# Diagonal softmax on one core: the first load split by partitions, an early normalization, one store fewer

## Chip, core and metric

The kernel runs on one core of a Trainium2 chip. The metric is the device time of one execution in microseconds (us). Lower is better.

## The reference

`x` and `y` are float32 tensors of shape 8 x 4096 x 512. For each of the 8 batches the reference takes the diagonal of `x @ y.T`, that is 4096 dot products of 512 elements, and a softmax over those 4096 numbers.

```python
gram = np.matmul(x, y.transpose(0, 2, 1))
diag = np.diagonal(gram, axis1=1, axis2=2)
diag = diag - diag.max(axis=-1, keepdims=True)
exp = np.exp(diag)
return (exp / exp.sum(axis=-1, keepdims=True)).astype(np.float32)
```

Only the diagonal is needed, so the kernel forms 32,768 dot products and no matrix product. Its inputs are 2 x 67.1 MB, its output is 0.13 MB.

## The kernel before

**Tiling.** Four batches make a "set"; there are two sets. Within a set each batch takes 32 partitions, so partition `p` holds 128 consecutive rows of one batch, as `C = 128` columns of a set. A step takes `R = 32` of these columns: one tile of 128 partitions x 32 rows x 512 elements of `x`, and the same of `y`. A partition's part of such a tile is 64 KB that lie next to each other in memory; the tile is 8.39 MB. Steps 0 to 3 cover the first set and steps 4 to 7 the second.

**Buffers.** There are two tiles for `x` (`xs[0]` and `xs[1]`, used in turn), one for `y` (`ys`), and a small one, `side`, to which ScalarE (ACT) copies the last `K = 6` rows of `ys`.

**A step of the main loop** (`t` = 0 to 5). The SP queue issues the loads of `x` (line 63) and of `y` (line 66). Line 123 has ACT copy the last six rows of `y` to `side`. VectorE (DVE) multiplies the first 26 rows in place (line 70, `products`), then the six rows from `side` (line 70 again), and sums 30 of the 32 rows (line 73). ACT sums the other two (line 78). `ys` is free for the next `y` as soon as the first product and ACT's copy are done; an `xs` tile is free when the sums are done.

**The softmax of a set.** `exps` takes each partition's largest dot product (line 97), the largest over the batch's 32 partitions (line 91), and the exponentials with their sums on ACT (line 104). `normalize` adds up those sums over the batch (line 91), takes the reciprocal (line 110) and scales `res` (line 111). The exponentials of the first set come at the end of step 3. Its `normalize` stands in step 4, between the first and the second product.

**The end.** Step 6 loads `y` in two halves; step 7 loads `x` and `y` in pieces of 16, 8, 4, 2 and then 1 rows and forms its dot products row by row on DVE (line 83). Line 156 then stores the first set from the SP queue in five pieces, of 32, 32, 32, 16 and 16 partitions. ACT's queue stores the second set with line 158, which is the last thing that the kernel does.

**Order.** The schedule is written out by hand: each engine's instructions run in the order of the program. SP issues 31 transfers and ACT one. Each transfer takes the next of eight completion semaphores in turn, so a transfer is also held until the one eight places ahead of it has landed.

Of the kernel before, what the change touches and what calls it, by code (L numbers as in the profile page):

```python
# [1 line left out]

# [5 lines left out]


@with_exitstack
def kernel(
    ctx: ExitStack,
    tc: tile.TileContext,
    x: bass.AP,
    y: bass.AP,
    out: bass.AP,
):
    nc = tc.nc
    ctx.enter_context(tc.manual_schedule())  # L20
    f32 = mybir.dt.float32
    Alu = mybir.AluOpType
    Act = mybir.ActivationFunctionType
    X = mybir.AxisListType.X
    B, N, D = x.shape
    P = nc.NUM_PARTITIONS
    G = 32
    Q = P // G
    C = N // G
    R = 32  # L30
    H = R // 2
    K = 6
    W = 2
    S = B // Q * (C // R)


    xv = x.rearrange("(s b) (j c) d -> s (b j) c d", b=Q, j=G)
    yv = y.rearrange("(s b) (j c) d -> s (b j) c d", b=Q, j=G)
    ov = out.rearrange("(s b) (j c) -> s (b j) c", b=Q, j=G)

    big = ctx.enter_context(tc.tile_pool(name="big", bufs=1))
    small = ctx.enter_context(tc.tile_pool(name="small", bufs=1))


    xs = [big.tile([P, R, D], f32, name=f"xs{i}") for i in range(2)]
    ys = big.tile([P, R, D], f32, name="ys")
    side = big.tile([P, K, D], f32, name="side")

    diag = [small.tile([P, C + i], f32, name=f"diag{i}") for i in range(B // Q)]
    res = [small.tile([P, C], f32, name=f"res{i}") for i in range(B // Q)]  # L50

    def columns(t, r0, n):
        c0 = t % (C // R) * R + r0
        return slice(c0, c0 + n)

    def rows(t, r0, n):
        return xs[t % 2][:, r0 : r0 + n, :]

    def dots_of(t, r0, n):
        return diag[t * R // C][:, columns(t, r0, n)]  # L60

    def load_x(t, r0, n):
        nc.sync.dma_start(out=rows(t, r0, n), in_=xv[t * R // C, :, columns(t, r0, n), :])  # L63

    def load_y(t, r0, n):
        nc.sync.dma_start(out=ys[:, r0 : r0 + n, :], in_=yv[t * R // C, :, columns(t, r0, n), :])  # L66

    def products(t, r0, n, yt):
        xt = rows(t, r0, n)
        nc.vector.tensor_tensor(out=xt, in0=xt, in1=yt, op=Alu.mult)  # L70

    def sums(t, r0, n):
        nc.vector.tensor_reduce(out=dots_of(t, r0, n), in_=rows(t, r0, n), axis=X, op=Alu.add)  # L73

    def sums_act(t, r0, n):
        for r in range(r0, r0 + n):
            row = xs[t % 2][:, r, :]
            nc.scalar.activation(out=row, in_=row, func=Act.Copy, accum_out=dots_of(t, r, 1))  # L78

    def dots(t, r0, n):  # L80
        for r in range(r0, r0 + n):
            xt = xs[t % 2][:, r, :]
            nc.vector.scalar_tensor_tensor(  # L83
                out=xt, in0=xt, scalar=1.0, in1=ys[:, r, :], op0=Alu.mult, op1=Alu.mult,
                accum_out=dots_of(t, r, 1),
            )

    def over_quadrant(name, column, op, negate=False):

        got = small.tile([P, 1], f32, name=name)  # L90
        nc.vector.tensor_reduce(  # L91
            out=got, in_=column.to_broadcast([P, G]), axis=X, op=op, negate=negate, apply_transpose=True
        )
        return got

    def largest(out, d):
        nc.vector.tensor_reduce(out=out, in_=d, axis=X, op=Alu.max)  # L97

    def exps(i, d):
        mxp = small.tile([P, 1], f32, name=f"mxp{i}")  # L100
        largest(mxp, d)
        nmx = over_quadrant(f"nmx{i}", mxp, Alu.max, negate=True)
        sump = small.tile([P, 1], f32, name=f"sump{i}")
        nc.scalar.activation(out=res[i], in_=diag[i][:, :C], func=Act.Exp, bias=nmx, scale=1.0, accum_out=sump)  # L104
        return sump

    def normalize(i, sump):
        total = over_quadrant(f"sum{i}", sump, Alu.add)
        rc = small.tile([P, 1], f32, name=f"rc{i}")
        nc.vector.reciprocal(out=rc, in_=total)  # L110
        nc.vector.tensor_single_scalar(out=res[i], in_=res[i], scalar=rc, op=Alu.mult)  # L111

    nc.vector.addr_align(128, offset=0, max_nops=0)
    nc.scalar.addr_align(128, offset=0, max_nops=0)
    nc.sync.drain()  # L117
    nc.sync.drain()  # L118

    for t in range(S - 2):  # L120
        load_x(t, 0, R)
        load_y(t, 0, R)
        nc.scalar.activation(out=side, in_=ys[:, R - K :, :], func=Act.Copy)  # L123
        products(t, 0, R - K, ys[:, : R - K, :])
        if t == C // R:
            normalize(0, sump)
        products(t, R - K, K, side)
        sums(t, 0, R - W)
        sums_act(t, R - W, W)
        if t == C // R - 1:  # L130
            sump = exps(0, diag[0])

    t = S - 2
    load_x(t, 0, R)
    for r0 in (0, H):
        load_y(t, r0, H)
        products(t, r0, H, ys[:, r0 : r0 + H, :])
    sums(t, R - H // 2, H // 2)
    sums_act(t, 0, R - H // 2)

    t += 1
    r0 = 0
    for n in (16, 8, 4, 2, 1, 1):
        if r0 < R - 1:
            load_x(t, r0, max(n, 2))
        load_y(t, r0, n)
        if r0 == R - 2:
            largest(diag[1][:, C:], diag[1][:, : C - 2])
        dots(t, r0, n)
        r0 += n  # L150

    met = small.tile([P, C - R], f32, name="met")
    nc.scalar.activation(out=met, in_=diag[1][:, : C - R], func=Act.Copy)  # L153

    for p, n in ((0, G), (G, G), (2 * G, G), (3 * G, G // 2), (3 * G + G // 2, G // 2)):
        nc.sync.dma_start(out=ov[0, p : p + n, :], in_=res[0][p : p + n, :])
    normalize(1, exps(1, diag[1][:, C - 2 :]))
    nc.scalar.dma_start(out=ov[1], in_=res[1])


# [1 line left out]
_INS = ['x', 'y']  # L162
_OUTS = [((8, 4096), 'float32')]


# [23 lines left out]
```

## Time and profile before

| What | Value |
|---|---|
| Median of 3 runs | 320.84 us (320.61 to 320.96) |
| The profiled execution's own time | 320.94 us |
| Its span in the profile | 319.2 us |
| VectorE busy | 244.7 us (77%) |
| ScalarE busy | 42.0 us (13%) |
| SP's transfer queue (q1), share of 16 DMA engines' span | 97.7% |
| Read from HBM | 134.22 MB, 421 GB/s over the span |
| Instructions | 305 |

The span runs from the first recorded event of the program to the last, and 1.74 us of the execution's time lie outside it. "Busy" is the time in which an engine had an instruction running. A DMA queue's share is the time that its packets took on the 16 DMA engines, over 16 spans. Times inside the span are counted from its start.

### The profile page before, as it was taken

Reading aid. Unit: us, or ns where it says so; the run is one execution under the profiler, and the core shown is the slowest. Engines: PE = TensorE matmul, PEld = TensorE weight load, DVE = VectorE, ACT = ScalarE, POOL = GpSimd, SP = SyncE. Lnnn points to the kernel's source line nnn. Section 1 sums busy time; section 2 is a strip of 40 time slices with the busy share of each in tenths; the row PEclk is TensorE's granted clock in tenths of the full one; section 3 lists DMA queues with packets and bytes.
Section 4 is the critical chain, followed back from the end, with each engine's and each line's share of the span. In section 5 each row is a group of like instructions: output and inputs, shape, how many; then the busy total and the mean of one; then the engine's idle time right before and its main releaser. Section 6 shows DMA issues by size and latency. Waiting matters only on the chain.

```text
span 319.2 us, 305 instructions
## 1 busy us (share of the span) xinstructions
DVE 244.7 (77%) x96; ACT 42.0 (13%) x84; POOL 0.2 (0%) x4
## 2 busy tenths in 40 slices
DVE  0000069995799949999399994999949999996995
ACT  1000030100301003010020103001030100197000
POOL 0000000000000000000000000000000000000000
DMA  9999999999999999999999999999999899999993
GB/s 372 419 394 476 444 394 460 452 402 394 501 419 394 476 444 394 427 485 402 394 501 419 394 476 444 394 452 460 402 394 485 382 435 435 427 435 413 421 413 113
DMA packets 4098, 134.37 MB, mean 421 GB/s; under 512 B 512, under 2 KB 768, under 8 KB 1408
## 3 DMA queue, kind: packets, MB, share of 16 engines
q1 hardware_dynamic: 3952, 134.29, 97.7%
q10 hardware_dynamic: 144, 0.07, 0.1%
q14 instruction: 2, 0.02, 0.0%
HBM read 134.22 MB, written 0.13 MB: 421 GB/s over the span
## 4 chain that ended last, share of the span: by engine, by line
DMA 62%; DVE 35%; issue 2%; SPq 0%; ACT 0%; DVEq 0%
DMA ys<-in_y_dram 62%; DVE xs L70 30%; DVE diag L73 4%; DVE xs L83 0%; SPq L63 0%; DVE res L111 0%; DVE sum L91 0%; DVE nmx L91 0%; ACT res L104 0%; DVE rc L110 0%; DVE mxp L97 0%; DVEq L70 0%; SPq L66 0%; SPq L118 0%; SPq L117 0%
## 5 line engine op out<-in xcount | busy, mean ns | idle before, releaser
L70 DVE TENSOR_TENSOR xs<-xs,ys 128x13312 f32<-128x13312 f32 (+1 forms) x8 | 101.4, 12689 | 67.6 <-DMA ys<-in_y_dram 67.6
L73 DVE TENSOR_REDUCE diag<-xs 128x30 f32<-128x15360 f32 (+1 forms) x7 | 101.3, 14477 | 0.2
L78 ACT ACTIVATE xs<-xs 128x512 f32<-128x512 f32 x36 | 22.2, 616 | 111.7 <-DVE xs L70 111.7
L123 ACT ACTIVATE side<-ys 128x3072 f32<-128x3072 f32 x6 | 16.6, 2763 | 123.6 <-DMA ys<-in_y_dram 123.6
L83 DVE SCALAR_TENSOR_TENSOR xs<-xs,ys 128x512 f32<-128x512 f32 x32 | 20.0, 686 | 3.2 <-DMA ys<-in_y_dram 3.2
L70 DVE TENSOR_TENSOR xs<-xs,side 128x3072 f32<-128x3072 f32 x6 | 20.1, 3352 | 0.0
L78 ACT ACTIVATION_READ_ACCUMULATOR xs<-xs 128x1 f32 x36 | 6.7, 186 | 0.0
L104 ACT ACTIVATE res<-diag,nmx 128x128 f32<-128x128 f32 x2 | 0.8, 402 | 37.5 <-DVE nmx L91 37.5
L83 DVE DVE_READ_ACCUMULATOR xs<-xs,ys 128x1 f32 x32 | 2.6, 81 | 0.0
L123 ACT ACT_TABLE_LOAD x1 | 1.3, 1283 | 1.2 <-PEq L173 1.2
L91 DVE TRANSPOSE_TENSOR_REDUCE sum<-sump 128x1 f32<-128x32 f32 x2 | 0.4, 208 | 0.6 <-ACT res L104 0.6
L111 DVE TENSOR_SCALAR res<-res,rc 128x128 f32<-128x128 f32 x2 | 0.6, 288 | 0.1
L97 DVE TENSOR_REDUCE mxp<-diag 128x1 f32<-128x128 f32 (+1 forms) x2 | 0.4, 221 | 0.1
L91 DVE TRANSPOSE_TENSOR_REDUCE nmx<-mxp 128x1 f32<-128x32 f32 x2 | 0.4, 211 | 0.1
L110 DVE RECIPROCAL rc<-sum 128x1 f32<-128x1 f32 x2 | 0.3, 164 | 0.1
L104 ACT ACTIVATION_READ_ACCUMULATOR res<-diag,nmx 128x1 f32 x2 | 0.4, 187 | 0.0
L97 DVE TENSOR_REDUCE diag<-diag 128x1 f32<-128x126 f32 x1 | 0.3, 284 | 0.1
L153 ACT ACTIVATE met<-diag 128x96 f32<-128x96 f32 x1 | 0.3, 283 | 0.0
L173 POOL MEMSET const-bfloat16-1.0<- 128x1 bf16 x1 | 0.1, 103 | 0.0
L173 POOL MEMSET const-uint8-127<- 128x1 uint8 x1 | 0.1, 102 | 0.0
L173 POOL MEMSET const-float32-0.0<- 128x1 f32 x1 | 0.1, 100 | 0.2 <-issue 0.2
L173 POOL MEMSET const-float32-1.0<- 128x1 f32 x1 | 0.1, 99 | 0.0
## 6 DMA issues: line engine op xcount, KB each, us to landing
ys<-in_y_dram SPq DMA_DIRECT2D x3, 4096.0 KB, 16.0
xs<-in_x_dram SPq DMA_DIRECT2D x1, 4096.0 KB, 14.9
xs<-in_x_dram SPq DMA_DIRECT2D x1, 2048.0 KB, 20.5
ys<-in_y_dram SPq DMA_DIRECT2D x1, 2048.0 KB, 17.2
xs<-in_x_dram SPq DMA_DIRECT2D x1, 1024.0 KB, 19.3
ys<-in_y_dram SPq DMA_DIRECT2D x1, 1024.0 KB, 21.3
xs<-in_x_dram SPq DMA_DIRECT2D x2, 512.0 KB, 22.9
ys<-in_y_dram SPq DMA_DIRECT2D x1, 512.0 KB, 22.9
```

Source lines behind the costliest of these rows:

```text
L70: nc.vector.tensor_tensor(out=xt, in0=xt, in1=yt, op=Alu.mult)
L73: nc.vector.tensor_reduce(out=dots_of(t, r0, n), in_=rows(t, r0, n), axis=X, op=Alu.add)
L78: nc.scalar.activation(out=row, in_=row, func=Act.Copy, accum_out=dots_of(t, r, 1))
L83: nc.vector.scalar_tensor_tensor(out=xt, in0=xt, scalar=1.0, in1=ys[:, r, :], op0=Alu.mult, op1=Alu.mult, accum_out=dots_of(t, r, 1),)
L91: nc.vector.tensor_reduce(out=got, in_=column.to_broadcast([P, G]), axis=X, op=op, negate=negate, apply_transpose=True)
L97: nc.vector.tensor_reduce(out=out, in_=d, axis=X, op=Alu.max)
L104: nc.scalar.activation(out=res[i], in_=diag[i][:, :C], func=Act.Exp, bias=nmx, scale=1.0, accum_out=sump)
L110: nc.vector.reciprocal(out=rc, in_=total)
L111: nc.vector.tensor_single_scalar(out=res[i], in_=res[i], scalar=rc, op=Alu.mult)
L123: nc.scalar.activation(out=side, in_=ys[:, R - K :, :], func=Act.Copy)
L153: nc.scalar.activation(out=met, in_=diag[1][:, : C - R], func=Act.Copy)
L173: nc = _bacc.Bacc("TRN2", target_bir_lowering=False, num_devices=1)
```

## The change

The load of `x` for step 0 becomes two transfers from SP: 16 partitions (0 to 15), then the other 112. The first set's `normalize` moves ahead of step 4's first product. The first set is stored in four pieces of 32 partitions, where it was three of 32 and two of 16. The number of transfers stays 32.

```diff
     for t in range(S - 2):
-        load_x(t, 0, R)
+        if t:
+            load_x(t, 0, R)
+        else:
+
+            for p, n in ((0, 16), (16, P - 16)):
+                nc.sync.dma_start(out=xs[0][p : p + n], in_=xv[0, p : p + n, :R, :])
         load_y(t, 0, R)
         nc.scalar.activation(out=side, in_=ys[:, R - K :, :], func=Act.Copy)
-        products(t, 0, R - K, ys[:, : R - K, :])
         if t == C // R:
             normalize(0, sump)
+        products(t, 0, R - K, ys[:, : R - K, :])
         products(t, R - K, K, side)
...
-    for p, n in ((0, G), (G, G), (2 * G, G), (3 * G, G // 2), (3 * G + G // 2, G // 2)):
+    for p, n in ((0, G), (G, G), (2 * G, G), (3 * G, G)):
         nc.sync.dma_start(out=ov[0, p : p + n, :], in_=res[0][p : p + n, :])
```

In the changed file lines 123, 156 and 158 become 128, 161 and 163, and the two transfers of step 0's `x` are line 126.

## The prediction

> **What bounds the kernel now.** I read the DMA part of the page first, because the kernel reads 134 MB and does little with each byte.
>
> ```profile
> DMA  9999999999999999999999999999999899999993
> q1 hardware_dynamic: 3952, 134.29, 97.7%
> HBM read 134.22 MB, written 0.13 MB: 421 GB/s over the span
> ```
>
> Every slice but the last has the 16 DMA engines busy. Next comes the chain that ended last, in order of time (start, length, what):
>
> ```profile
> 1.28 41.38 DMA ys<-in_y_dram
> 42.77 14.04 DVE xs L70
> 56.88 24.49 DMA ys<-in_y_dram
> ...
> 294.40 19.24 DMA ys<-in_y_dram
> 313.66 1.36 DVE xs L83 x4
> ```
>
> The chain names DVE for 35%, but no transfer waits for it. The timeline of SP's queue shows why:
>
> ```profile
> 0.83 0.39 SPq L63 DMA_DIRECT2D xs<-in_x_dram  x1
> 1.28 0.42 SPq L66 DMA_DIRECT2D ys<-in_y_dram  x1
> 1.75 0.43 SPq L63 DMA_DIRECT2D xs<-in_x_dram  x1
> 56.88 0.33 SPq L66 DMA_DIRECT2D ys<-in_y_dram  x1
> 76.32 0.33 SPq L63 DMA_DIRECT2D xs<-in_x_dram  x1
> ...
> 304.19 7.86 SPq L156 DMA_DIRECT2D out_dram<-res  x5
> ```
>
> Step 1's x, issued at 1.75, takes 60.3 to land (the longest x in the view of that tensor), so until 62.05. Step 1's y was issued at 56.88, 5.2 ahead of that, and lands at 81.37; step 2's x was issued at 76.32, 5.05 ahead. The engines always hold the next work. One tile lasts 81.37 - 62.05 = 19.3, or 8.39 MB / 19.3 = 434 GB/s. So a microsecond that the slowest DMA engine loses anywhere is a microsecond at the end, and time that DVE gains is not.
>
> The trace's single DMA packets tell more. A partition's row of a tile is one packet of 65,536 bytes, and in the steady part it takes 2.42, which is 27.1 GB/s for one engine and 433 for 16. The engines start one after another: the first packets begin between 1.87 and 3.13 and take 2.66 to 3.31, so they end between 4.85 and 5.94. From there each engine's packets follow with no gap. By the last 64 KB packets the order of the engines is another: single slow packets, of up to 2.96 near 235, have moved some of the early ones back.
>
> [...] 496 packets of 4 bytes, 31 transfers by 16, and at the end the last engine has 2, 2, 2, 1 and 1 packets of 512 bytes for the five stores. So 16 partitions put one row on each of 16 engines, and 112 put seven. [...] Nothing in this trace shows a large load to so few partitions[...].
>
> **The change, part by part.**
>
> *Normalization moved.* It is three DVE instructions, 0.21 + 0.16 + 0.29 = 0.66:
>
> ```profile
> 193.07 0.40 ACT L104 ACTIVATE res<-diag,nmx 128x128 f32<-128x128 f32 x1 [15.55 <-DVE nmx L91]
> 193.38 0.19 ACT L104 ACTIVATION_READ_ACCUMULATOR res<-diag,nmx 128x1 f32 x1
> 197.57 14.03 DVE L70 TENSOR_TENSOR xs<-xs,ys 128x13312 f32<-128x13312 f32 x1 [4.59 <-DMA ys<-in_y_dram]
> 211.51 0.21 DVE L91 TRANSPOSE_TENSOR_REDUCE sum<-sump 128x1 f32<-128x32 f32 x1
> ```
>
> It now runs from about 193.6, when ACT's sums are there, to 194.3, in the 4.59 in which DVE waits for step 4's y. Behind it in DVE's order stands only that product, which y holds anyway. It leaves the stretch from 211.51 to 212.15, so the release of step 6's x, issued at 231.76, comes 0.64 earlier, but y is in flight until 236.2: nothing gained. Cost 0; without the idle stretch it would be at most 0.66 of DVE time inside the 5 us lead, still 0.
>
> *Stores.* One issue of 0.31 on SP goes. SP's stores wait for loads eight places back and stand behind the last loads in the engines' order; the end is set by the second set's store (ACT, issued 316.77, landing after 1.6). Per engine one semaphore packet of 0.009 goes. The bounds are -0.1 and +0.1; I take 0. The semaphores shift by one for all later loads, with the extra one in front, so no load waits for another one than before. The first product waits for a third semaphore, at most 0.05 within the 5 us lead.
>
> *The split.* SP issues one transfer more, about 0.45 from start to start, ahead of step 0's y and step 1's x. Both then queue behind 19 us of x, so 0. What counts is the engines:
>
> - Gain: with one row per engine, later engines need not wait while eight rows are set up for earlier ones, if that is what staggers them. It is at most 5.94 - 4.85 = 1.09, at least 0.
> - Loss in the first transfer: [...] A packet then takes 4 x 2.42 = 9.68 in place of 2.42, +7.3 for every engine[...] since DMA is the limit to the end, this is never made up.
> - Loss in the second: seven rows per engine. If they are consecutive (partitions 16 + 7e to 22 + 7e for engine e)[...]. The trace shows no 112-partition load: bounds 0 and 9.7, and I take 4.8.
>
> [...] 7.3 + 4.8 - 1.0 (the stagger vanishes in packets of 9.7) = +11.1. The profiled execution took 320.94 (span 319.2 and 1.74 around it), so 332.0, and 0.1 less against the median of the runs: 331.9. This case's own range is 326.5 to 338: 7.3 - 1.1 at the low end[...].
>
> **Rivals.**
>
> - *The engines bind[...]: not slower.* Place: the first transfer. If 16 packets to partitions 0 to 15 take about 3 as before, only the gain is left. Of the 1.09, late packets in mid-run hide part: I take 0.4, so 320.4, range 319.8 to 321.2. For it: 27.1 GB/s is as well an engine's rate, and the stores from 32 partitions run at the same 27 ns a packet as the last store from 128. Against: those are 512 bytes each[...]. It decides from a first packet under about 3.5 us.
> [...]
> - *Rows dealt in turn.* If the 112 rows go to engines one at a time, [...] x takes 77 in place of 19: about 378. A 128-partition load dealt so would run at a quarter of what the trace shows, so this is unlikely.
> - *The split does not act*: if DMA had slack, any of this would be hidden. The SP timeline excludes it.
>
> **Chances.** [...] rows in turn 0.03, engine-bound 0.36. About 0.2% (0.64 us) is what a measurement of this kernel tells from no change. Engine-bound splits into 0.12 faster, 0.21 within, 0.03 slower[...]. In all: faster 0.12, same 0.21, slower 0.67. The range must reach down to the engine-bound case[...]: 319.9 to 338.0, leaving out about 0.1.
>
> **What would show it.** Right: the chain's first piece, step 0's y, ends near 53 in place of 42.67, all later pieces are shifted by the same amount, first packets take near 9.7, and the first slices of the GB/s row fall far below 372. Then DVE busy stays at 244.7 and its idle time before line 70 grows by some 11. The normalization shows at some 194 plus the shift. Wrong: first packets of about 3 and step 0's y landing near 42[...].

## The result and the profile after

The changed kernel takes 341.92 us (median of 6 runs, 341.5 to 342.2); beside it the kernel before took 320.73 us (6 runs, 320.46 to 320.96). The ratio is 1.066, with a 95% interval of 1.0646 to 1.0673: 21.2 us slower. The sign was forecast, the size was not: 331.9 was said, with 338.0 as the upper end.

The DMA part of the page of the changed kernel:

```profile
DMA  9989989898999999999999999999999999999992
GB/s 125 246 239 246 239 377 485 377 485 377 485 385 470 400 462 400 462 400 454 416 447 416 454 431 439 408 454 408 454 424 447 416 408 435 431 431 412 426 411 102
q1 hardware_dynamic: 3952, 134.29, 97.7%
HBM read 134.22 MB, written 0.13 MB: 395 GB/s over the span
```

The bytes and packets are the ones of before, and the engines are as "busy" as before: 97.7%, now of a longer span. What tells is the GB/s row: its first five slices are 125 to 246, where they were 372 to 476 in the kernel before:

```profile
GB/s 372 419 394 476 444 394 460 452 402 394 501 419 394 476 444 394 427 485 402 394 501 419 394 476 444 394 452 460 402 394 485 382 435 435 427 435 413 421 413 113
```

A DMA engine counts as busy while its packet is slow: in experiment 3 the DMA share is 0.94 at 111 GB/s, where the kernel before has 1.00 at 434.

The windows view shows the same in rates (the last column; the one ahead of it is the DMA share). It counts a packet in the window in which it starts, so that a short window has some error. First the kernel before, then the changed one:

```profile
2.00:10.00 8.00, 0.00 (x0) 0.44 (x1) 0.00 (x0) 1.00 1.06 435
11.00:40.00 29.00, 0.00 (x0) 0.00 (x0) 0.00 (x0) 1.00 1.00 434
60.00:300.00 240.00, 211.72 (x44) 37.41 (x80) 0.00 (x0) 1.00 1.00 432
```

```profile
2.00:10.00 8.00, 0.00 (x0) 0.44 (x1) 0.00 (x0) 1.00 0.90 115
11.00:40.00 29.00, 0.00 (x0) 0.00 (x0) 0.00 (x0) 1.00 0.92 224
60.00:300.00 240.00, 210.82 (x25) 25.43 (x33) 0.00 (x0) 1.00 1.00 431
```

So there is a stretch at about a quarter of the rate (the 16 partitions), a longer one at about half (the 112), and from 60 us on nothing has changed. The chain that ended last, of the changed kernel:

```profile
0.80 63.10 another core or an unknown queue
...
64.03 14.04 DVE xs L70
78.07 0.02 SPq L66
...
78.14 24.46 DMA ys<-in_y_dram
...
315.66 19.20 DMA ys<-in_y_dram
...
334.96 1.32 DVE xs L83 x4
```

The first piece carries the name of no transfer; the waits view names the one that came last (waits in total, their number, the longest). First the kernel before, then the changed one:

```profile
DVE xs L70 <- DMA ys<-in_y_dram: 67.6, 6, 42.8
```

```profile
DVE xs L70 <- DMA ys<-in_y_dram: 88.1, 6, 64.0
```

The longest of these waits was 42.8 and is 64.0. The first product starts at 64.03 where it started at 42.77, the last dots at 334.96 where they started at 313.66: 21.26 and 21.30. The whole loss is there before the first product.

The timeline of the changed kernel around step 4 shows the moved normalization:

```profile
214.58 0.19 ACT L104 ACTIVATION_READ_ACCUMULATOR res<-diag,nmx 128x1 f32 x1
214.80 0.21 DVE L91 TRANSPOSE_TENSOR_REDUCE sum<-sump 128x1 f32<-128x32 f32 x1 [0.62 <-ACT res L104]
215.04 0.16 DVE L110 RECIPROCAL rc<-sum 128x1 f32<-128x1 f32 x1
215.24 0.28 DVE L111 TENSOR_SCALAR res<-res,rc 128x128 f32<-128x128 f32 x1
218.83 14.03 DVE L70 TENSOR_TENSOR xs<-xs,ys 128x13312 f32<-128x13312 f32 x1 [3.31 <-DMA ys<-in_y_dram]
```

It lies in DVE's idle time, which ends with step 4's y as before.

The trace names no engine for a packet, but a packet starts where the one ahead of it on its engine ends, so the packets can be put in 16 rows. The single 64 KB packets, averaged over the 16 engines by their place in the order (us):

| Packet of an engine | before | after |
|---|---|---|
| 1st (in the split: the transfer of 16) | 2.96 | 8.40 |
| 2nd to 8th, added up (the transfer of 112) | 16.94 | 30.95 |
| these seven one by one, after the change | | 5.24, 4.78, 3.27, 3.80, 4.50, 4.75, 4.60 |
| 9th (the first of step 0's y) | 2.42 | 3.16 |
| 10th to 16th, each | 2.42 | 2.42 |

That is +5.4, +14.0 and +0.7, together 20.2 (before rounding) in the mean of the engines. The slowest engine ends y at 63.35 where it ended at 42.22, +21.1; the engines have also come further apart.

### The profile page after: what moved, and what is told of

It is laid out like the page before. It is cut to its first block, busy times and chain, and to the rows that moved or that the text cites. A ratio compares the mean times of both kernels' runs of the same rounds, so it can differ in the third digit from the quotient of the medians.

```text
span 340.4 us, 306 instructions
## 1 busy us (share of the span) xinstructions
DVE 244.7 (72%) x96; ACT 42.0 (12%) x84; POOL 0.2 (0%) x4
## 3 DMA queue, kind: packets, MB, share of 16 engines
q1 hardware_dynamic: 3952, 134.29, 97.7%
## 4 chain that ended last, share of the span: by engine, by line
DMA 46%; DVE 32%; another core or an unknown queue 19%; issue 2%; ACT 0%; DVEq 0%; SPq 0%
DMA ys<-in_y_dram 46%; DVE xs L70 28%; DVE diag L73 3%; DVE xs L83 0%; DVE res L111 0%; DVE nmx L91 0%; DVE sum L91 0%; ACT res L104 0%; DVE rc L110 0%; DVE mxp L97 0%; DVEq L70 0%; SPq L66 0%; DVEq L115 0%; DVEq L83 0%
```

## The experiments

The kernels change the part that loads step 0's x; all else is as in the changed kernel unless it is said. The times of the kernel before beside them were 320.55 to 320.76. Experiments 1 and 2 rest on 4 to 12 runs each, those from 3 on on one run each, and these are read by their packets as well as by their times. In the expectations theory P says that the partitions which a transfer writes set its pace, theory H that the rows which it reads do.

**1. Which of the three edits it is.** The split taken back, the other two edits kept:

```diff
-        if t:
-            load_x(t, 0, R)
-        else:
-
-            for p, n in ((0, 16), (16, P - 16)):
-                nc.sync.dma_start(out=xs[0][p : p + n], in_=xv[0, p : p + n, :R, :])
+        load_x(t, 0, R)
```

> The changed kernel with step 0's x in one transfer again; the moved normalization and the four stores stay. Theory 'the split is the whole loss': within 0.5 us of the kernel before (320.7). Rival 'the moved normalization or the stores have a share': above 321.5.

Measured: 320.59 us against 320.55, ratio 0.9998 (0.9989 to 1.0007). The moved normalization and the four stores together change nothing that can be measured.

And the split alone, put into the kernel before (the same `if`, with the normalization and the five stores of before):

> The kernel before with the split of step 0's x alone: the normalization stays between the two products and the stores stay five. If the split is the whole loss: 341.9, as the changed kernel. If the other two edits hide or add anything beside it: off by more than 0.5 us.

Measured: 341.74 us, ratio 1.0655 (1.0638 to 1.0673). The split is the whole loss.

**2. A second transfer by itself.** The same number of transfers, but cut along the rows of the tile, so that both reach all 128 partitions:

```diff
-            for p, n in ((0, 16), (16, P - 16)):
-                nc.sync.dma_start(out=xs[0][p : p + n], in_=xv[0, p : p + n, :R, :])
+            for r, n in ((0, 4), (4, R - 4)):
+                load_x(t, r, n)
```

> Step 0's x in two transfers again, but cut along the rows of the tile: 4 of the 32 rows for all 128 partitions, then the other 28. Theory P: [...] within 0.6 us of the kernel before (320.6). Rival 'a second transfer in front costs by itself': above 322.

Measured: 320.72 us against 320.66, ratio 1.0003 (0.9995 to 1.0012). One more transfer in front costs nothing; it is the cut by partitions that does.

**3. Destination or source.** Step 0's x in eight transfers of 16 consecutive partitions (from here on the diffs show only the added lines; they stand in place of the two lines of the split):

```diff
+            for p in range(0, P, 16):
+                nc.sync.dma_start(out=xs[0][p : p + 16], in_=xv[0, p : p + 16, :R, :])
```

> Step 0's x in eight transfers of 16 consecutive partitions. Theory P[...]: every packet takes about 8.3 us as the first 16 did in the changed kernel, 66 us for this x in place of 19.4, so about 321 + 47 = 368. Theory H (source rows at a pitch of 256 KB collide in memory): the same here. Rival 'only the first transfer of a program is slow': about 327 or less.

The same with partitions eight apart, at both ends:

```diff
+            for p in range(8):
+                nc.sync.dma_start(out=xs[0][p::8], in_=xv[0, p::8, :R, :])
```

> Step 0's x in eight transfers of 16 partitions that stand eight apart (0, 8, 16, ... then 1, 9, ...); the source rows are then 2 MB apart. Theory P: [...] packets of about 4.3 us, 34 us for this x, total about 336. Theory H: no relief by the destination; with the source further apart at a power of two, packets of 8 us or more, total 365 or more, or, if the wider pitch happens to be good, 2.4 us and 321.

And the source rows of the second with the destinations of the first:

```diff
+            for p in range(8):
+                nc.sync.dma_start(out=xs[0][16 * p : 16 * p + 16], in_=xv[0, p::8, :R, :])
```

> Eight transfers to 16 consecutive partitions, but from source rows 2 MB apart, so that rows of x land in other partitions than those of y and the output is another one. Theory P: like eight consecutive transfers, packets of about 8.3 us, total about 368. Theory H: like the spread transfers, whatever these take.

Measured: 374.73, 342.19 and 375.83 us. The windows view of the three, in this order, over most of the stretch in which x is loaded:

```profile
11.00:75.00 64.00, 0.00 (x0) 0.00 (x0) 0.00 (x0) 1.00 0.94 111
```

```profile
8.00:42.00 34.00, 0.00 (x0) 0.00 (x0) 0.00 (x0) 1.00 0.92 191
```

```profile
11.00:75.00 64.00, 0.00 (x0) 0.00 (x0) 0.00 (x0) 1.00 0.96 110
```

With other source rows and the same destinations the rate is the same, 111 and 110; with the same source rows and other destinations it is 191. So the partitions written decide. After the first, packets take 9.20 us with 16 consecutive partitions (9.29 with the other source rows) and 4.9 to 5.1 with the spread ones. All three totals come out 6 to 8 us above the expectations; the 8.3 us in two of them had been taken from the first packets of a program, which are shorter (8.40 in the mean, in the changed kernel). 16 packets in 9.20 us are 114 GB/s, about a quarter of the 433 of packets of 2.42.

**4. Halves.** Two transfers of 64 partitions:

```diff
+            for p in range(0, P, 64):
+                nc.sync.dma_start(out=xs[0][p : p + 64], in_=xv[0, p : p + 64, :R, :])
```

> Step 0's x in two transfers of 64 partitions. Theory P: [...] packets of 4.8 to 5.1 us, 39 to 41 us for this x in place of 19.4, total 340 to 342. Rival 'only transfers of 16 or of an odd 112 are slow': 321 to 323.

Measured: 341.85 us, most packets 5.12. The windows view of this run:

```profile
8.00:42.00 34.00, 0.00 (x0) 0.00 (x0) 0.00 (x0) 1.00 0.90 185
```

The view has 185 in a window of few packets; 16 packets in 5.12 us are 205, about half of 433. Two transfers of disjoint halves cost 21 us for one tile here.

**5. Which rows of the 112 go to which engine.** Call the packets that have the same place in the order on all 16 engines a round. If engine e has the seven consecutive partitions from 16 + 7e, its first rows are partitions 16, 23, ..., 121, its second ones 17, 24, ..., and so on. These sets, each named by its first partition, can be loaded one by one:

```diff
+            nc.sync.dma_start(out=xs[0][0:16], in_=xv[0, 0:16, :R, :])
+            for p in range(16, 23):
+                nc.sync.dma_start(out=xs[0][p::7], in_=xv[0, p::7, :R, :])
```

> Partitions 0 to 15 as in the changed kernel, then the other 112 in seven transfers of 16, of every seventh partition (16, 23, ..., 121, then 17, 24, ... and so on). Theory C (in the 112-partition load engine e has the seven consecutive rows from 16 + 7e, so these seven transfers are its seven rounds): the same packet times round by round, about 5.3, 4.7, 3.0, 3.7, 4.4, 4.7, 4.5[...]; total about 342. Rival 'the rows are dealt in another order': a different pattern, and a total that differs by several us.

Measured: 341.93 us, against 341.92 for the changed kernel. The mean packets of the seven rounds are 5.27, 4.67, 3.33, 3.73, 4.61, 4.65 and 4.46, the pattern of the changed kernel. This fits rows dealt in runs of seven that follow each other. The two short rounds are sets 18 and 19, and in the changed kernel two engines stand out in each: in the third round of the 112 they take 4.79 and 4.81 beside 2.68 to 3.31 of the other fourteen, in the fourth two others take 4.41 and 4.42 beside 3.59 to 3.73. Call such two engines a slow pair. A load of all 128 partitions can't be dealt in such runs: with eight consecutive partitions for each engine its rounds would be the sets of partitions eight apart of experiment 3, which took 4.9 to 5.1, and its packets take 2.42.

The same destinations with other source rows (`in_=xv[0, 16 + 16 * p : 32 + 16 * p, :R, :]` for the set that begins at 16 + p):

> The same destinations as in the run with seven transfers of every seventh partition, but the source rows of each of the seven are 16 that follow each other (so x stands in other partitions than y and the output is another one). Theory 'the destinations decide': the same packet times round by round, total about 342. Rival 'in these rounds memory decides': another pattern, total off by several us.

Measured: 342.66 us, with the same pattern (mean packets of 5.35, 4.69, 3.28, 3.86, 4.67, 4.73 and 4.59). Here too the destinations decide.

**6. Who pays beside the slow pair.** Transfers of 96 and 32 partitions (`((0, 96), (96, 32))` in place of `((0, 16), (16, P - 16))`):

> Step 0's x in transfers of 96 and 32 partitions. Theory C with slowed bystanders[...]: six rounds[...], about 4.5 us each, then two rounds[...], 4.8 to 5.1: 37 us for this x, total about 338. Rival [...] the colliding engines alone take 4.84 in a round, the others 2.42, and most engines get through the first six rounds in under 20 us.

Measured: 340.82 us. From the second round on every engine's packets take 4.8 to 5.1, where about 4.5 was expected up to the sixth; no engine keeps 2.42.

Is that so with one slow pair as well? In the step-7 runs the rounds of sets 18 and 19 had followed two in which all engines are slow (means of 5.27 and 4.67). So three tiles (step 0's x and y, step 1's x) were loaded set by set, each set three times in a row, sets 18 and 19 first. Of the edit, the loads that take the place of these three tiles' own:

```diff
+            for p in (18, 19, 16, 17, 20, 21, 22):
+                nc.sync.dma_start(out=xs[0][p::7], in_=xv[0, p::7, :R, :])
+                nc.sync.dma_start(out=ys[p::7], in_=yv[0, p::7, :R, :])
+                nc.sync.dma_start(out=xs[1][p::7], in_=xv[0, p::7, R : 2 * R, :])
+            nc.sync.dma_start(out=xs[0][0:16], in_=xv[0, 0:16, :R, :])
+            nc.sync.dma_start(out=ys[0:16], in_=yv[0, 0:16, :R, :])
+            nc.sync.dma_start(out=xs[1][0:16], in_=xv[0, 0:16, R : 2 * R, :])
```

> The tiles of step 0's x and y and step 1's x each in seven transfers of every seventh partition and one of 16 consecutive, ordered so that the same set of 16 partitions is loaded three times in a row: first the two sets[...] (18 and 19)[...], then partitions 0 to 15. Theory 'bystanders are slowed': also in a second and third round of one set, [...] total about 320.6 + 3 x 21.2 = 384. Rival '[...] the long packets of the others were carried over from the round before': the others fall to 2.42 in second and third rounds, and one pair alone is left at 4.8.

Measured: 402.08 us. The total is 18 above 384 because step 1's x now lands before the first product starts, at 125.5: nothing is left in the queue until the next y is issued at 139.6, and the page's GB/s row falls to 13 and 0 in two slices. The packets answer the question against the first theory, as far as one slow pair goes. In the second and third round of set 18, fourteen engines take 2.42 us and only one pair 4.88 and 4.95. But then the fourteen go on to set 19, while that pair is still on set 18: now two pairs are slow at once, and the twelve others take 4.1 a packet, until the first pair is through at 16.8; the next packet takes 2.47, and only set 19's own pair still needs 4.9.

The same with set 16 in front, `(16, 18, 19, 17, 20, 21, 22)`:

> As the run that loads each set of 16 partitions three times in a row, but the first set is 16, 23, ..., 121, [...] nothing is carried over from an earlier set. Theory 'two pairs at once slow every engine': the twelve engines [...] take about 4.1 to 4.9 us in the second and third round too. Rival 'it was the mixture of two sets that slowed them': they take 2.42 in the second and third round[...]. Total about 400 either way.

Measured: 402.23 us. In the second and third round of set 16 all sixteen engines take 5.01; when they come to set 18, fourteen of them fall to 2.43. The windows view shows it: first the run that begins with set 18 (5 to 9.5 us), then the one that begins with set 16 (6 to 15 us).

```profile
5.00:9.50 4.50, 0.00 (x0) 0.00 (x0) 0.00 (x0) 1.00 1.08 437
```

```profile
6.00:15.00 9.00, 0.00 (x0) 0.00 (x0) 0.00 (x0) 1.00 1.12 233
```

The second window is short; 16 packets in 5.01 us are 209 GB/s. Set 18 alone costs its own pair (the others 2.42), set 19 alone does too (the others 2.47), and both at once bring the twelve others to 4.1: here it is the number of slow pairs that counts, not which one. Whether set 16 holds two such pairs is not shown: at 5.01 for all sixteen none stands out. Why the others are held up is open: no trace here shows the path between an engine and the partitions it writes.

## Why the prediction was right and wrong

- *DMA sets the end, and lost time is not made up*: right. 21.26 us late at the first product, 21.30 at the last dots, and 431 GB/s in between. "No transfer waits for it" is put too short, though: in the kernel before, SP's line 66 waits 160.1 us for DVE before it issues the loads of y. What holds is that they are issued some 5 us (5.2 for step 1's) before the DMA engines get to them.
- *Normalization and stores, 0*: right, 0.9998 for both together. So was the extra transfer on SP, by the cut along rows.
- *The transfer of 16, +7.3*: right in direction, and experiment 3 puts the loss on the partitions written (9.20 us a packet, 9.29 from other rows). The factor of four behind the 9.68 was the author's estimate, which no trace of before showed. The size was +5.4: the first packet of a program already took 2.96 before, not 2.42, and to partitions 0 to 15 it took 8.4, less than the 9.68 and than the 9.2 of later packets to 16 consecutive partitions.
- *The 112 partitions, +4.8 with 9.7 as the bound*: this is the step that failed; it measured +14.0. The rows seem to be dealt as was assumed (experiment 5). The 4.8 and the 9.7 are two and four packets of 2.42, the author's estimate, which was not shown; it let most packets of an engine take 2.42. In five of the seven rounds none does (means of 4.50 to 5.24, no packet under 4.15), and a pair that is still in the round before slows the others of the next too (to 4.1 in experiment 6). Seven packets then take 31.0, close to seven at half rate (7 x 4.84 = 33.9), and this bound should have been the upper one: 7.3 + 16.9 would have held the result. A second slip was to take the most common engine's 4.8: by the prediction's own rule the slowest engine counts, and its bound for that one was 9.7. The sum would then have been +16.0, still 5 short.
- *The stagger of the start, -1.0*: nothing was gained. First packets began between 1.86 and 3.74 with the split, between 1.84 and 2.83 in the run of the split alone, and between 1.86 and 2.62 with one load, whose time is that of the kernel before. The stagger of one execution was no property of the kernel.
- *Not in the sum*: y's first packet, 0.7 longer behind the mixed transfers, and about 1 us by which the slowest engine lost more than the mean.
- *The range*: its low end doesn't follow from the terms given: 7.3 - 1.1 leads to 327.0 and not 326.5. The 338 at the high end was the author's estimate; the result lies beyond it.
- *The rivals*: an engine-bound load is out by first packets of 8.4 us, where it had to stay under about 3.5. Rows dealt in turn are out by 341.92 us against 378, and by experiment 5. The prediction put the end of the chain's first piece near 53; it came at 63.9.

## What to carry to other kernels

Where transfers set the time, cut a load along the free dimension and keep all 128 partitions in each piece: the cut by rows cost nothing, the same bytes cut by partitions cost 20 to 55 us a tile here, 16 + 112 as much as 64 + 64. When you estimate a load cut by partitions, don't let a part of the engines run at full rate: take the pace of the slow ones (here 4.8 to 5.1 us a packet in place of 2.42, and 9.2 with 16 consecutive partitions) for all as the upper bound. And read the GB/s row beside the busy share of the DMA engines, which stayed at 97.7%.

## What was not expected of the hardware

- In the second and third round of set 18 fourteen engines kept 2.42 us a packet and two took 4.88 and 4.95; in those of set 16 all sixteen took 5.01.
- Packets of 65,536 bytes took 9.20 us to 16 consecutive partitions, 3.8 times the 2.42 of a load of all 128 (7.1 GB/s an engine in place of 27.1). The slow pair of set 18 and the halves, at 4.88 to 5.12 us (13.4 to 12.8 GB/s an engine), took a little over twice 2.42.
- The first packets to 16 consecutive partitions were shorter in the changed kernel: 8.4 us, where the following ones of experiment 3 took 9.2. The engines began up to 1.9 us apart, so the early ones had less company at first; whether that is all was not tested.
